# The feed-forward of a two-layer decoder step as a seven-product block form with its hidden values in DRAM, and a recurrence with one difference per level

## The chip, the core and the metric

The kernel is one inference step for 1024 prompt tokens and 8 sample tokens, in fp32, on one core of a Trainium2 chip. A core has five engines that run side by side, each with its own queue that is worked strictly in order: TensorE (PE: matmuls, with weight loads shown as PEld), VectorE (DVE), ScalarE (ACT), GpSimd (POOL) and SyncE (SP, which here only issues DMAs). They wait for each other by semaphores. The metric is device time in microseconds (us) of one execution; lower is better.

## The reference

The step has four parts: a gated linear recurrence (HGRN2), a feed-forward, latent attention (MLA), a second feed-forward. Each sits between two RMS norms.

```python
def swiglu(h, w_in, w_out):               # h is normed x: (1032, 1024)
    g, u = jnp.split(h @ w_in, 2, axis=-1)  # w_in: (1024, 2*2816)
    return (jax.nn.silu(g) * u) @ w_out     # w_out: (2816, 1024)

def hgrn2_mixer(h, s0, lb, w_in, g_norm, w_out):
    q, fz, i, gz = jnp.split(h @ w_in, 4, axis=-1)
    q = jax.nn.silu(heads(q)) * (DK_A ** -0.5)
    log_f = jnp.logaddexp(log_lb, jnp.log1p(-lbh) + jax.nn.log_sigmoid(heads(fz)))
    log_f = jnp.minimum(log_f, 0.0)
    k = -jnp.expm1(log_f)
    o, s = hgrn2_chunked(q, k, v, log_f, s0, ...)  # decays exp(b_t - b_s), b = cumsum(log_f)
    ...

for l in range(2):                        # mixer: HGRN2 in layer 0, MLA in layer 1
    x = x + rmsnorm(mixer(rmsnorm(x, g[0])), g[1])
    x = x + rmsnorm(swiglu(rmsnorm(x, g[2]), w_ffn_in[l], w_ffn_out[l]), g[3])
```

## The kernel before

**Layout.** Features lie on the 128 partitions, tokens along the free dimension. The 1032 tokens are three spans of 344 (`NS`, `W`). An fp32 product is made of three matmuls of halves in fp32r (`mm3`, L172 to 179: high x high, high x low, low x high), so each operand is split into a rounded half (a ScalarE copy) and a rest (a subtraction), for weights in `weight` (L132), for activations in `split` (L127) and `put_x` (L213).

**Feed-forward** (`ffn`, L533). For each of 22 chunks of 128 hidden columns, `inp` makes g and u for each span (8 blocks of 1024 features x 3 matmuls each, L550 and L554), multiplies by the rows' norm factor r *behind* the product (L552, L556), applies silu, multiplies (L557) and splits the result. The output product (`out_chunk`, L593) of the chunk before follows, and VectorE adds it to `acc` (L582). The last three chunks' output products stand in `outf`, together with the input product of the very last chunk, and there the closing norm runs along behind.

**Between two parts** (`finish`, L296). While the products of span s are made, `norm` of the span before it works: a first statistic `r1`, then per block of 128 features: acc times gain and r1 (L324), plus the old x that comes by DMA as `xs` (L325), the new x split as input of the next part (`put_x`), its square for the next norm factor. Then `first` gives four products of the next part that are made ahead (L360 to 363). The next part's factor r is not needed for them, since it is applied behind the product.

**Recurrent layer** (`hgrn`, L727). Eight heads, each with four projections (`proj`), the logarithm of the gate (L806 to 820), and a recurrence over blocks (`rec`). In `scaled` (L866), for each half of the tokens and each of seven levels, two differences to a reference go to VectorE (L874, L875), one exponential to ScalarE (L876) and a product to GpSimd and VectorE each (L877, L878). Projections of one head and the recurrence of the head before are dealt out by counters (`KN['pace']`).

**What sets the order.** Instructions are recorded in program order and then ordered engine by engine by a scheduler with a timeline of its own; a queue, once written, is not reordered on the chip. Tiles come from pools, and a tile that takes over a buffer waits for the buffer's last reader.

## Time and profile before

| | |
|---|---|
| median of 3 runs | 2951.73 us (2948.17 to 2955.06) |
| the profiled execution: time, span | 2951.07 us, 2949.3 us |
| TensorE | 2806.7 us busy, 95% of the span |
| weight loads | 2635.9 us, 89% |
| VectorE | 1770.6 us, 60% |
| ScalarE | 1091.2 us, 37% |
| GpSimd | 993.0 us, 34% |
| granted TensorE clock, mean | 0.976 of full speed |

The parts follow each other: the recurrent layer and its output projection to some 785 us, the first feed-forward to some 1468, then attention, the second feed-forward from some 2200 to the end. Shares over the whole span mix stages with different limits; they are read by stage. Matmuls are pipelined, so the pitch of a stream of them is read from their starts, not from their durations.

### The profile page before, as it was taken

Reading aid. Unit: us, or ns where it says so; the run is one execution under the profiler, and the core shown is the slowest. Engines: PE = TensorE matmul, PEld = TensorE weight load, DVE = VectorE, ACT = ScalarE, POOL = GpSimd, SP = SyncE. Lnnn points to the kernel's source line nnn. Section 1 sums busy time; section 2 is a strip of 40 time slices with the busy share of each in tenths; the row PEclk is TensorE's granted clock in tenths of the full one; section 3 lists DMA queues with packets and bytes.
Section 4 is the critical chain, followed back from the end, with each engine's and each line's share of the span. In section 5 each row is a group of like instructions: output and inputs, shape, how many; then the busy total and the mean of one; then the engine's idle time right before and its main releaser. Section 6 shows DMA issues by size and latency. Waiting matters only on the chain.

```text
span 2949.3 us, 54597 instructions
## 1 busy us (share of the span) xinstructions
PE 2806.7 (95%) x22360; PEld 2635.9 (89%) x22360; DVE 1770.6 (60%) x3505; ACT 1091.2 (37%) x2245; POOL 993.0 (34%) x912
## 2 busy tenths in 40 slices
PE   7988888899999999999999999978999999999998
PEld 7888888888799999999969899946889999999998
DVE  8888888873634444444357788795353444444535
ACT  6555555564431111111144666523443111111112
POOL 3455445551532322333332111242153333223330
PEclk9999999999999999999999999989999999999999
DMA  5122222144311111111132111496431111111112
GB/s 182 50 62 67 67 61 66 60 159 132 113 51 51 51 44 44 47 48 51 43 94 77 51 48 51 158 349 235 142 106 44 51 51 46 49 44 43 51 57 95
DMA packets 230970, 242.51 MB, mean 82 GB/s; under 512 B 19074, under 2 KB 211120, under 8 KB 224704
## 3 DMA queue, kind: packets, MB, share of 16 engines
q1 hardware_dynamic: 205456, 170.14, 18.9%
q0 software_dynamic: 7456, 43.00, 3.9%
q10 hardware_dynamic: 17808, 25.89, 2.5%
q8 instruction: 176, 2.88, 0.4%
q14 instruction: 74, 0.61, 0.1%
HBM read 194.87 MB, written 44.12 MB: 81 GB/s over the span
## 4 chain that ended last, share of the span: by engine, by line
PE 75%; DVE 14%; ACT 5%; issue 4%; POOL 1%; DMA 1%; SPq 0%; DVEq 0%; ACTq 0%; POOLq 0%
PE ps L177 22%; PE ps L178 22%; PE ps L179 22%; PE ps L252 2%; PE ps L1459 1%; DVE E L875 1%; DVE X L878 1%; PE ps L1386 1%; DVE E L874 1%; DVE turned L1459 1%; DVE b L826 1%; PE ps L198 1%; DVE qe L927 1%; ACT sig L830 1%; ACT w L151 1%
## 5 line engine op out<-in xcount | busy, mean ns | idle before, releaser
L177 PE MATMUL ps<-xh,w 128*128 128x344 f32 x3360 | 1105.5, 329 | 2.0 <-ACT xh L221 1.9
L178 PE MATMUL ps<-xl,w 128*128 128x344 f32 x3360 | 1084.8, 323 | 1.6 <-DVE xl L222 1.6
L179 PE MATMUL ps<-xh,w 128*128 128x344 f32 x3360 | 1080.3, 322 | 0.0
L155 POOL TENSOR_TENSOR w<-raw,w 128x512 fp32r<-128x512 f32 (+1 forms) x360 | 469.5, 1325 | 818.6 <-ACT w L151 798.9
L177 PEld LDWEIGHTS ps<-xh,w 128*128 128x128 f32 x3360 | 640.4, 191 | 25.1 <-issue 11.1
L178 PEld LDWEIGHTS ps<-xl,w 128*128 128x128 f32 x3360 | 640.5, 191 | 15.2 <-issue 8.8
L179 PEld LDWEIGHTS ps<-xh,w 128*128 128x128 f32 x3360 | 639.4, 190 | 6.0 <-issue 5.6
L582 DVE TENSOR_TENSOR acc<-ps,acc 128x344 f32<-128x344 f32 x864 | 397.5, 513 | 0.0
L151 ACT CAST w<-raw 128x1024 fp32r<-128x1024 f32 (+4 forms) x206 | 206.2, 1002 | 425.3 <-PE ps L179 325.1
L177 PE MATMUL ps<-gh,w 128*128 128x344 f32 x1056 | 338.8, 323 | 0.6 <-ACT gh L129 0.3
L179 PE MATMUL ps<-gh,w 128*128 128x344 f32 x1056 | 338.5, 321 | 0.0
L178 PE MATMUL ps<-gl,w 128*128 128x344 f32 x1056 | 338.1, 320 | 0.0
L557 POOL TENSOR_TENSOR u<-u,a 128x344 f32<-128x344 f32 x132 | 122.5, 929 | 532.8 <-DVE u L556 528.2
L556 DVE TENSOR_TENSOR u<-ps,r 128x344 f32<-128x344 f32 x132 | 68.1, 516 | 388.6 <-PE ps L179 388.4
L129 ACT CAST gh<-u 128x344 fp32r<-128x344 f32 x132 | 63.5, 481 | 504.0 <-POOL u L557 504.0
L552 DVE TENSOR_TENSOR a<-ps,r 128x344 f32<-128x344 f32 x132 | 68.1, 516 | 232.8 <-PE ps L179 226.8
L177 PEld LDWEIGHTS ps<-gh,w 128*128 128x128 f32 x1056 | 198.4, 188 | 5.6 <-issue 1.7
L178 PEld LDWEIGHTS ps<-gl,w 128*128 128x128 f32 x1056 | 198.8, 188 | 1.1 <-DVE gl L130 0.8
L179 PEld LDWEIGHTS ps<-gh,w 128*128 128x128 f32 x1056 | 198.8, 188 | 1.1 <-issue 1.1
L130 DVE TENSOR_TENSOR gl<-u,gh 128x344 fp32r<-128x344 f32 x132 | 70.1, 531 | 150.9 <-ACT gh L129 150.9
L553 ACT ACTIVATE a<-a 128x344 f32<-128x344 f32 x132 | 64.5, 490 | 224.1 <-DVE a L552 223.9
L877 POOL TENSOR_TENSOR X<-lin,E 128x256 f32<-128x256 f32 x112 | 108.9, 977 | 79.2 <-ACT E L876 48.4
(376 smaller groups left out, 4090.9 us busy)
## 6 DMA issues: line engine op xcount, KB each, us to landing
raw<-in_w_ffn_in_dram SPq DMA_DIRECT2D x88, 512.0 KB
raw<-in_w_ffn_out_dram SPq DMA_DIRECT2D x44, 512.0 KB
raw<-in_w_in_a_dram SPq DMA_DIRECT2D x32, 512.0 KB
xs<-x_d SPq DMA_DIRECT2D x72, 172.0 KB
x_d<-acc ACTq DMA_DIRECT2D x9, 1376.0 KB
x_d<-y SPq DMA_DIRECT2D x3, 1376.0 KB
od_a<-oh ACTq DMA_DIRECT2D x24, 172.0 KB
od_a<-ol ACTq DMA_DIRECT2D x24, 172.0 KB
```

Source lines behind the costliest of these rows:

```text
L130: (lo_eng or self.nc.vector).tensor_tensor(out=lo, in0=src, in1=hi, op=ALU.subtract)
L151: nc.scalar.copy(wh[:, :n], raw[:, :n])
L155: eng.tensor_tensor(out=wl[:, sl], in0=raw[:, sl], in1=wh[:, sl], op=ALU.subtract)
L177: nc.tensor.matmul(out, lhsT=wh, rhs=ah, start=first and i == 0, stop=False)
L178: nc.tensor.matmul(out, lhsT=wh, rhs=al, start=False, stop=False)
L179: nc.tensor.matmul(out, lhsT=wl, rhs=ah, start=False, stop=last and i == n - 1)
L552: nc.vector.tensor_tensor(out=a, in0=pg, in1=r[s], op=ALU.mult)
L553: nc.scalar.activation(out=a, in_=a, func=AF.Silu)
L556: nc.vector.tensor_tensor(out=u, in0=pu, in1=r[s], op=ALU.mult)
L557: nc.gpsimd.tensor_tensor(out=u, in0=u, in1=a, op=ALU.mult)
L582: nc.vector.tensor_tensor(out=acc[s][:, dc, :], in0=po, in1=acc[s][:, dc, :], op=ALU.add)
L877: nc.gpsimd.tensor_tensor(out=Xl[:, :, 0, :], in0=kl[:, :, 0, :], in1=El[:, :, 0, :], op=ALU.mult)
```

## The change

**Feed-forward.** `Gated` makes g and u from one 2 x 2 block form. The rows of a weight chunk are the halves of the 1024 features, and its two column blocks are the gate's and the up part's 128 columns, so A11, A12 (gate) and A21, A22 (up); the tokens come as two pairs of 2 x 258 (`HT`, `Q`), so B11 to B22. Seven block products (`PRODUCTS`) with sums of blocks replace eight. The weight sums S1 to S4 are made on GpSimd for each chunk; the token differences T1 to T4 and the splits of all seven token blocks are made once (`tokens`). Since blocks are mixed, x is normed *before* it is split: `put_half` writes gain x r x acc into `xn`, and `finish` makes no product ahead (`halves`). A visit is one chunk with one or both pairs: three chunks first with pair 0 alone, 19 with both, the three again with pair 1 alone. Products accumulate in two PSUM banks per pair, whose partial sums are copied out between products. The hidden values go to DRAM (`g_d`); when all are made, the output product reads them back and takes two chunks in one accumulation (`GROUP`).

**Recurrence.** `scaled` makes one difference per level, and the two signs come from two exponentials. The gate's logarithm takes six ScalarE operations and three on VectorE per half, instead of four and seven. Two small copies go to ScalarE, and the negation of f goes into a scale.

```diff
@@ finish @@
+    def put_half(s, r):
+        for pair in range(2):
+            lo, hi = max(s * W, pair * HT), min((s + 1) * W, (pair + 1) * HT)
...
+            for c in range(KC):
...
+                nc.vector.scalar_tensor_tensor(out=to, in0=acc[s][:, c, fr], scalar=g_next[:, c:c + 1], in1=r[:, fr], op0=ALU.mult, op1=ALU.mult)
...
-            xs = pool.tile([P, W], F32, name="xs", tag="xs", bufs=6)
+            xs = pool.tile([P, W], F32, name="xs", tag="xs", bufs=4 if halves else 6)
...
-            k.put_x(s, c, y, g_next)
-            if not last:
+            if not halves:
+                k.put_x(s, c, y, g_next)
+            if not last or halves:
                 s2.add(acc[s][:, c:c + 1, :], None, xs)
...
             rs[s] = yield from s2.rstd(k.new_r(s))
+            if halves:
+                yield from put_half(s, rs[s])
...
-    for i, m in enumerate(first):
+    for i, m in enumerate(() if halves else first):
@@ the new input product @@
+PRODUCTS = (("A11", "B11"), ("S1", "T1"), ("S2", "T2"), ("S4", "B22"), ("S3", "T3"), ("A12", "B21"), ("A22", "T4"))
+class Gated:
...
+        self.visits = [(f, (0,)) for f in early] + [(f, both) for f in range(len(early), NF)] + [(f, (1,)) for f in early]
...
+    def make(self, v):      # seven weight blocks of a visit
+        for i in range(2):
+            raw = k.wp.tile([P, 1024], F32, name="raw", tag="raw", bufs=2)
...
+        def total(to, a, b, op):
+            t = self.pool.tile([P, 512], F32, name="S", tag="S", bufs=2)
+            nc.gpsimd.tensor_tensor(out=t, in0=src[a], in1=src[b], op=op)
...
+            k.split(hi, lo, src[name])
...
+    def tokens(self, pair, places):
...
+            if name in how:
+                a, b = how[name]
+                nc.vector.tensor_tensor(out=src[name], in0=src[a], in1=src[b], op=ALU.subtract)
+            pool, tag = places.pop(0)
+            x = pool.tile([P, 2, KC // 2, Q], F32R, name="X", tag=tag)
+            k.split(x[:, 0], x[:, 1], src[name])
...
+    def visit(self, v, g_d):
...
+                k.mm3(to, terms, new, True, name in ("S2", "S4", "S3", "A22"))
+                if name == "A11":
+                    nc.scalar.copy(t1[p], A[p])
+                elif name == "S1":
+                    nc.scalar.copy(t5[p], C[p])
+                elif name == "S2":
+                    nc.scalar.copy(t2[p], A[p])
+                elif name == "S4":
+                    nc.vector.tensor_tensor(out=t2[p], in0=C[p], in1=t2[p], op=ALU.add)
+                    nc.scalar.activation(out=t2[p], in_=t2[p], func=AF.Silu)
+                elif name == "S3":
+                    nc.vector.tensor_tensor(out=t5[p], in0=A[p], in1=t5[p], op=ALU.add)
+                    nc.gpsimd.tensor_tensor(out=t5[p], in0=t5[p], in1=t2[p], op=ALU.mult)
+                    store(p, 1, t5[p])
...
+    def run(self, g_d):
...
+                    if v == 0:
+                        next(ta, None)
+                    elif v in (1, 2) and (v > 1 or i % 2):
+                        next(tb, None)
+                    self.ahead(v * NP_ + i + 5)
+                    next(steps)
@@ hgrn: the gate, per half @@
-                        nc.vector.scalar_tensor_tensor(out=t1, in0=x, scalar=-1.0, in1=x, op0=ALU.mult, op1=ALU.min)
-                        nc.scalar.activation(out=t1, in_=t1, func=AF.Exp)
+                        nc.scalar.activation(out=t1, in_=x, func=AF.Abs)
+                        nc.scalar.activation(out=t1, in_=t1, func=AF.Exp, scale=-1.0)
...
-                        nc.vector.tensor_scalar(out=t2, in0=t2, scalar1=hc(gt.l1), scalar2=hc(gt.loglb), op0=ALU.add, op1=ALU.max)
-                        nc.vector.tensor_tensor(out=t2, in0=t2, in1=t1, op=ALU.add)
+                        nc.vector.scalar_tensor_tensor(out=t2, in0=t2, scalar=hc(gt.loglb), in1=t1, op0=ALU.max, op1=ALU.add)
...
-                    nc.vector.tensor_scalar(out=f, in0=f, scalar1=-1.0, scalar2=None, op0=ALU.mult)
@@ rec: scaled @@
-                nc.vector.tensor_tensor(out=El[:, :, 0, :], in0=ref, in1=bl[:, :, 0, :], op=ALU.subtract)
-                nc.vector.tensor_tensor(out=El[:, :, 1, :], in0=bl[:, :, 1, :], in1=ref, op=ALU.subtract)
-                nc.scalar.activation(out=E, in_=E, func=AF.Exp)
+                nc.vector.tensor_tensor(out=pairs(E), in0=pairs(bv), in1=ref, op=ALU.subtract)
+                for i, sign in enumerate((-1.0, 1.0)):
+                    nc.scalar.activation(out=El[:, :, i, :], in_=El[:, :, i, :], func=AF.Exp, scale=sign)
...
-                nc.vector.tensor_copy(el, eb.rearrange("p (j n) -> p j n", j=CH)[:, :, P - 1])
+                nc.scalar.copy(el, eb.rearrange("p (j n) -> p j n", j=CH)[:, :, P - 1])
```

**What stands where.** TensorE's queue at the first feed-forward's entrance, before: xh and xl are the split inputs, ss the sums of squares of the last span.

```order
L177 MATMUL ps<-xh_81,w 128x344
L178 MATMUL ps<-xl_82,w 128x344
L179 MATMUL ps<-xh_81,w 128x344
L198 MATMUL ps<-ss_8832,one 128x344
L198 MATMUL ps<-ss_8840,one 128x344
L177 MATMUL ps<-xh_8041,w 128x344
L178 MATMUL ps<-xl_8042,w 128x344
```

TensorE's queue at the same place in the changed program, from the last matmul of the output projection on: sq and xs are squares for the two statistics, X the split token blocks.

```order
L184 MATMUL ps<-xh_8009,w 128x344
L257 MATMUL ps<-sq,one 32x344 x4
L257 MATMUL ps<-xs,one 32x344 x8
L203 MATMUL ps<-rs_m,one_72 128x344 x2
L257 MATMUL ps<-xs,one 32x344 x8
L203 MATMUL ps<-rs_m,one_72 128x344
L182 MATMUL ps<-X,w 128x258
L183 MATMUL ps<-X,w 128x258
```

Before, products of the feed-forward (xh, xl of another span) stand up to the last statistics; now nothing stands between the output projection and the statistics of two spans, and the first product of 258 columns comes behind them.

VectorE's queue at that place, before, from the last span's r1 on.

```order
L209 SCALAR_TENSOR_TENSOR rs_y<-rs_q,rs_y 128x344
L324 SCALAR_TENSOR_TENSOR acc<-acc,gains,rs_y 128x344 x8
L325 TENSOR_TENSOR acc<-acc,xs 128x344
L222 SCALAR_TENSOR_TENSOR xl_8042<-acc,gains,xh_8041 128x344
L325 TENSOR_TENSOR acc<-acc,xs 128x344
L222 SCALAR_TENSOR_TENSOR xl_8042<-acc,gains,xh_8041 128x344 x2
L336 TENSOR_TENSOR ss_8840<-ss_8840,xs 128x344
L222 SCALAR_TENSOR_TENSOR xl_8042<-acc,gains,xh_8041 128x344 x4
L336 TENSOR_TENSOR ss_8840<-ss_8840,xs 128x344
L222 SCALAR_TENSOR_TENSOR xl_8042<-acc,gains,xh_8041 128x344
L336 TENSOR_TENSOR ss_8840<-ss_8840,xs 128x344
L552 TENSOR_TENSOR a<-ps,r_8369 128x344
```

VectorE's queue in the changed program, from the last span's r1 on: xn is the normed input, written over by its differences.

```order
L214 SCALAR_TENSOR_TENSOR rs_y<-rs_q,rs_y 128x344
L133 TENSOR_TENSOR X<-xn,X 128x1032
L345 SCALAR_TENSOR_TENSOR acc<-acc,gains,rs_y 128x344 x8
L632 TENSOR_TENSOR xn<-xn 128x4x258
L346 TENSOR_TENSOR acc<-acc,xs 128x344 x2
L212 SCALAR_TENSOR_TENSOR rs_q<-rs_q,rs_m 128x344
L214 SCALAR_TENSOR_TENSOR r_8744<-rs_q,rs_y 128x344
L321 SCALAR_TENSOR_TENSOR xn<-acc,gains,r_8744 128x344 x8
L133 TENSOR_TENSOR X<-xn,X 128x1032 x2
L632 TENSOR_TENSOR xn<-xn 128x4x258
L133 TENSOR_TENSOR X<-xn,X 128x1032 x4
L133 TENSOR_TENSOR w<-S,w 128x512
```

Where the first use of the norm factor (a from ps and r) followed the last split, the second norm factor, eight multiplications and the wide splits now stand ahead of the first visit's fifth weight (w from S).

VectorE's queue at the gate of a head in the recurrent layer, before: tw is the gate's work tile.

```order
L810 SCALAR_TENSOR_TENSOR tw<-lin 128x516
L813 SCALAR_TENSOR_TENSOR tw<-lin,tw 128x516
L814 TENSOR_SCALAR tw<-tw,lb_580 128x516
L815 SCALAR_TENSOR_TENSOR tw<-tw 128x516
L818 TENSOR_SCALAR tw<-tw,lb_579,loglb 128x516
L793 TENSOR_TENSOR lin<-ps,r_543 128x344
L908 COPY_PREDICATED Ad_141<-lv,ps 128x128 x2
L819 TENSOR_TENSOR tw<-tw 128x516
L908 COPY_PREDICATED Ad_141<-lv,ps 128x128
L820 TENSOR_SCALAR b<-tw 128x516
```

The same place in the changed program.

```order
L1046 TENSOR_TENSOR X<-lin,E 128x256
L982 SCALAR_TENSOR_TENSOR tw<-lin,tw 128x516
L962 TENSOR_TENSOR lin<-ps,r_543 128x344
L986 SCALAR_TENSOR_TENSOR tw<-tw,loglb 128x516
L987 TENSOR_SCALAR b<-tw 128x516
L1076 COPY_PREDICATED Ad_141<-lv,ps 128x128
```

Four operations per half have left the queue, and the ones that remain take over their inputs.

## Rows read from the trace of the kernel before

**Rows 1.** windows view: us; busy PE, PEld, DVE, ACT, POOL; clock, DMA, GB/s

```profile
0.00:690.00 690.00, 610.70 (x6828) 566.61 (x6829) 573.57 (x1046) 377.04 (x684) 330.11 (x277) 0.94 0.30 93
...
785.00:795.00 10.00, 3.53 (x10) 2.33 (x9) 7.99 (x12) 4.01 (x6) 6.11 (x6) 0.67 0.35 123
...
795.00:1468.00 673.00, 672.79 (x4286) 672.50 (x4285) 295.37 (x622) 133.62 (x215) 216.67 (x187) 1.00 0.17 50
...
1468.00:1580.00 112.00, 106.34 (x563) 82.50 (x562) 70.55 (x115) 54.48 (x112) 36.40 (x31) 0.97 0.30 95
...
2193.00:2203.00 10.00, 3.49 (x8) 2.57 (x9) 7.63 (x12) 5.00 (x6) 5.98 (x6) 0.76 0.31 105
...
2203.00:2850.00 647.00, 647.00 (x4116) 647.00 (x4115) 289.64 (x612) 127.96 (x207) 204.57 (x179) 1.00 0.17 50
```

**Rows 2.** the same view, inside the first feed-forward.

```profile
1000.00:1400.00 400.00, 400.00 (x2550) 400.00 (x2550) 184.57 (x394) 71.10 (x107) 122.71 (x107) 1.00 0.16 47
```

**Rows 3.** the same view, one head of the recurrent layer.

```profile
203.04:279.14 76.10, 67.35 (x807) 62.50 (x807) 66.56 (x119) 40.92 (x74) 39.01 (x32) 0.96 0.22 65
```

**Rows 4.** timeline, 256-column products: start, duration, engine, line, operation.

```profile
1773.33 0.28 PE L178 MATMUL ps<-PTl,vh 128*128 128x256 f32 x1
...
1775.95 0.28 PE L179 MATMUL ps<-w,cl 128*128 128x256 f32 x1
...
1773.45 0.19 PEld L177 LDWEIGHTS ps<-PTh,vh 128*128 128x128 f32 x1
...
1773.57 0.19 PEld L178 LDWEIGHTS ps<-PTl,vh 128*128 128x128 f32 x1
```

**Rows 5.** weight preparation by line, 800 to 1400: busy us, mean ns, idle.

```profile
L151 ACT CAST w<-raw 128x1024 fp32r<-128x1024 f32 x54 | 56.9, 1055 | 168.0 <-PE ps L179 144.9 <-DMA raw<-in_w_ffn_in_dram 23.2
...
L155 POOL TENSOR_TENSOR w<-raw,w 128x512 fp32r<-128x512 f32 x107 | 136.4, 1296 | 208.7 <-ACT w L151 208.7
```

**Rows 6.** timeline at the second feed-forward's entrance, and one from 1512.

```profile
1512.87 1.29 DVE L155 TENSOR_TENSOR w<-raw,w 128x512 fp32r<-128x512 f32 x2 [0.56 <-ACT w L151]
...
2157.94 2.61 SPq L323 DMA_DIRECT2D xs<-x_d  x4
...
2177.20 0.74 PE L198 MATMUL ps<-rs_m,one 128*128 128x344 f32 x2
...
2180.63 6.71 DVE L324 SCALAR_TENSOR_TENSOR acc<-acc,gains,rs_y 128x344 f32<-128x344 f32 x8
...
2198.86 0.50 DVE L552 TENSOR_TENSOR a<-ps,r 128x344 f32<-128x344 f32 x1
...
2199.29 0.50 DVE L556 TENSOR_TENSOR u<-ps,r 128x344 f32<-128x344 f32 x1
```

**Rows 7.** VectorE by line, 0 to 690: count, busy us, mean ns, idle.

```profile
L874 DVE TENSOR_TENSOR E<-b 128x256 f32<-128x256 f32 x112 | 84.7, 756 | 4.1 <-POOL kt L925 1.2 <-POOL X L877 1.0
...
L875 DVE TENSOR_TENSOR E<-b 128x256 f32<-128x256 f32 x112 | 64.9, 579 | 0.0
...
L923 DVE TENSOR_TENSOR E<-b 128x512 f32<-128x512 f32 x16 | 16.8, 1048 | 0.0
...
L820 DVE TENSOR_SCALAR b<-tw 128x516 f32<-128x516 f32 x16 | 14.1, 878 | 0.0
...
L813 DVE SCALAR_TENSOR_TENSOR tw<-lin,tw 128x516 f32<-128x516 f32 x16 | 11.1, 692 | 12.9 <-ACT tw L812 12.9
...
L834 DVE SCALAR_TENSOR_TENSOR lin<-lin,sig 128x1032 f32<-128x1032 f32 x8 | 9.8, 1226 | 0.0
...
L973 DVE COPY qpad<-lin 128x8 f32<-128x8 f32 x8 | 7.0, 869 | 0.0
```

**Rows 8.** timeline of one weight load and its cast, 1013 to 1019.

```profile
1013.89 8.15 SPq L148 DMA_DIRECT2D raw<-in_w_ffn_in_dram  x2
...
1017.96 1.05 ACT L151 CAST w<-raw 128x1024 fp32r<-128x1024 f32 x1 [1.87 <-DMA raw<-in_w_ffn_in_dram]
```

**Rows 9.** windows view, same head, the gate's tile alone: VectorE, ScalarE.

```profile
203.04:279.14 76.10, 10.46 (x14) 5.08 (x8) 0.96 0.22 65
```

More of the change, by code (lines that the diff above doesn't have):

```diff
@@ L25 @@
 W = T // NS
+HT = T // 2
+Q = HT // 2
 FF = 2816
@@ L162, in open_pre, with mm3 @@
     def open_pre(self):
-        self.pre, pool = self.right("pre", 2)
-        return pool
+        self.pre = self.right("pre", 2)
+        return self.pre[1]
     def close_pre(self):
         if self.pre is not None:
-            self.pre.close()
+            self.pre[0].close()
             self.pre = None
-    def mm3(self, out, terms, first=True, last=True):
+    def mm3(self, out, terms, first=True, last=True, more=False):
         nc = self.nc
         n = len(terms)
+        skip = {"skip_group_check": True} if more else {}
         for i, ((wh, wl), (ah, al)) in enumerate(terms):
-            nc.tensor.matmul(out, lhsT=wh, rhs=ah, start=first and i == 0, stop=False)
-            nc.tensor.matmul(out, lhsT=wh, rhs=al, start=False, stop=False)
-            nc.tensor.matmul(out, lhsT=wl, rhs=ah, start=False, stop=last and i == n - 1)
+            nc.tensor.matmul(out, lhsT=wh, rhs=ah, start=first and i == 0, stop=False, **skip)
+            nc.tensor.matmul(out, lhsT=wh, rhs=al, start=False, stop=False, **skip)
+            nc.tensor.matmul(out, lhsT=wl, rhs=ah, start=False, stop=last and i == n - 1, **skip)
     def xterm(self, k, s):
@@ L302, in finish @@
     rs = [None] * NS
+    def put_half(s, r):
+        for pair in range(2):
+            lo, hi = max(s * W, pair * HT), min((s + 1) * W, (pair + 1) * HT)
+            if lo >= hi:
+                continue
+            if pair not in k.xn:
+                k.xn[pair] = [k.xpool[1].tile([P, KC // 2, HT], F32, name="xn", tag=f"x{i}{pair}") for i in "hl"]
+            for c in range(KC):
+                to = k.xn[pair][c // 4][:, c % 4, lo - pair * HT:hi - pair * HT]
+                fr = slice(lo - s * W, hi - s * W)
+                nc.vector.scalar_tensor_tensor(out=to, in0=acc[s][:, c, fr], scalar=g_next[:, c:c + 1], in1=r[:, fr], op0=ALU.mult, op1=ALU.mult)
+                if c % 2:
+                    yield
     def products(s):
@@ L338, in norm @@
         nc.scalar.dma_start(out=x_d[s], in_=acc[s])
-        if not last:
+        if not last or halves:
             for _ in range(lags[1]):
@@ new lines, in ffn, with fetch @@
+        gp = st.enter_context(tc.tile_pool(name="gp", bufs=2, reuse_waits="tile"))
+        G, wo = {}, {}
+        order = [*range(LAST, NF), *range(LAST)]
+        def fetch(n):
+            f = order[n]
+            if f not in G:
+                t = gp.tile([P, 2, T], F32R, name="G", bufs=4)
+                nc.sync.dma_start(out=t.bitcast(F32), in_=g_d[f])
+                for s in range(NS):
+                    G[f, s] = tuple(t[:, i, s * W:(s + 1) * W] for i in range(2))
+                G[f] = t
+                wo[f] = k.weight(w_out[f * P:(f + 1) * P, :].unsqueeze(1), 1, D, None, gp if n % 2 else None)
@@ new lines, in ffn @@
+        fetch(0)
+        fetch(1)
+        acc = [k.new_acc() if k.accs is not None and s < NS - 1 else accp.tile([P, KC, W], F32, name=f"acc{s}") for s in range(NS)]
+        k.x_tiles(k.xpool[1], range(NS - 1))
+        k.x_tiles(k.xpool2[1], [NS - 1])
+        f = 0
+        while f < NF - LAST:
+            fs = range(f, min(f + (GROUP if f else 1), NF - LAST))
+            for s in range(NS):
+                for dc in range(KC):
+                    if dc == 0 and s < 2:
+                        fetch(fs[-1] + 1 + s)
+                    po = out_chunk(k, wo, G, [order[n] for n in fs], s, dc)
+                    if f == 0:
+                        nc.scalar.copy(acc[s][:, dc, :], po)
+                    else:
+                        nc.vector.tensor_tensor(out=acc[s][:, dc, :], in0=po, in1=acc[s][:, dc, :], op=ALU.add)
+            f = fs[-1] + 1
@@ L584, in outf @@
+        for f in range(NF - LAST, NF):
+            fetch(f)
         def outf(s, dc):
-            if dc == 0:
-                next(units[NF - 1])
-            po = out_chunk(k, wo, G, range(NF - LAST, NF), s, dc)
+            po = out_chunk(k, wo, G, order[NF - LAST:], s, dc)
             nc.vector.tensor_tensor(out=acc[s][:, dc, :], in0=po, in1=acc[s][:, dc, :], op=ALU.add)
```

194 lines of the change are left out of this document (123 added, 71 removed).

## The prediction

> **What bounds the kernel now.** I read the busy time by stage first, then single stretches of the timeline. In [rows 1] TensorE is busy 672.8 of 673 us from 795 to 1468 and all 647 us from 2203 to 2850: these are the two feed-forwards, and nothing but TensorE's own pitch bounds them. [rows 2] gives the pitch of the 344-column products: 2550 matmuls in 400 us, 156.9 ns each. At both entrances TensorE stands: between 785 and 795 it ran 10 matmuls and between 2193 and 2203 only 8 [rows 1], where 64 fit, so each entrance loses about 8.5 us now. In the recurrent layer, 0 to 690, VectorE is the densest engine. One head there lasts 76.1 us, with VectorE busy 66.6, TensorE 67.4 (latencies counted), ScalarE 40.9 and GpSimd 39.0 [rows 3].
>
> **The products.** Per 128 hidden columns the old input product runs 2 x 3 x 8 x 3 = 144 matmuls of 344 columns: 144 x 0.1569 = 22.6 us. The new form runs 7 products x 2 token pairs x 4 x 3 = 168 matmuls of 258 columns. The nearest row is the 256-column product of the attention: 23 starts from 1773.33 to 1775.95, 2.62 us for 22 steps, 119.1 ns [rows 4]; two more columns at the slope between the two widths (37.8 ns for 88) make 120.0. So 20.2 us. A layer has 3696 such matmuls for 3168: 443.5 for 497.1 us, twice -53.6 = **-107**. The output product keeps its 1584 matmuls of 344.
>
> The load of a matrix lasts 0.19 us, starts while a matmul runs, and the next starts 0.12 us later [rows 4], so loads lie under each other and under matmuls. The Trainium skill (TensorE: Matmul & The Clock Gate, The mechanism) says that a load overlaps a running matmul only where they use different row groups. By that rule loads would be paid on top of the streams and the -107 would be lost, 3020 where the rows give 2913; the trace disagrees.
>
> **Inside a two-pair visit** (19 a layer, 20.2 us each) the other engines have room. ScalarE: 7 casts of 512 (half of the 1.06 us in [rows 5]) and 14 small copies, casts and Silus of 258 at some 0.4: 9.5 us. VectorE: 7 subtractions of 512 at 0.65 and 12 of 258 at some 0.4: 9.4. GpSimd: 4 weight sums at 1.30 [rows 5] and two products at some 0.75: 6.7. A bank that is added to again rests three products, 4.3 us, while a copy takes 0.4. I charge 0.15 us a visit for single late copies, **+6**; from 0 (it only adds waits) to the price in the slower rival.
>
> **The entrance of the feed-forward** is where the gain goes back. Today x is multiplied by the weights before the norm is known: the old queue goes from the last xl to r's first use, and the matmuls of chunks 0 and 1 fill TensorE meanwhile. Now x must be normalised first, split and differenced, and all of that stands on VectorE. By the order of the changed program, the second pass over span 1 starts only at the end of the output projection. Behind that end VectorE has:
> - span 1: eight multiplications, 6.7 us as now [rows 6]; the last four additions wait for xs buffers (4, not 6), which the statistics must have read and a load of 2.6 us [rows 6] must refill; then statistics and rstd, of which 3.4 us are seen from its matmul at 2177.20 to the next multiplication [rows 6]. About 14.
> - 16 half-width multiplications at 0.25 (0.43 for 344 back to back in [rows 6], less 172 columns), three operations over 1032 columns at 1.2 (L834 in [rows 7]), two small ones: 8.5.
> - span 2: 6.7, one of 1.2, two additions, and the same tail, later, because one addition stands behind all eight multiplications: 18.
> - eight multiplications (3.4), seven operations of 1032 (8.4), three weight subtractions (2.0; two halves took 1.29 in [rows 6]): 14.
>
> That is 54.5 us until the first visit's fifth weight is there. Visits 1 and 2 then put ten operations of 1032, eleven of 512 and eleven of 258 on VectorE: 12 + 7.2 + 4.7 = 24, to 79, and TensorE has three products (4.3) behind them: 83 us for work of 252 x 0.12 = 30.2. Lost 53, less today's 8.5: +44 an entrance, **+88**. Low end: both tails hidden, 16 less each, +56. High end: the 22 wide operations at the crowded rate, as L874 with 0.76 on average against 0.43 for a wider one alone [rows 6, 7], +0.8 each: +123.
>
> **Smaller terms.** The last three one-pair visits take 84 x 0.12 = 10.1 us, but the way from one visit's last weight to the next one's is a load of 4.1 us [rows 8], four GpSimd sums in a row (5.2) and some 3 us of casts and subtractions: 12.2. Two of them show it in each layer: **+8** (0 to 20). From the last input product to the first output product the hidden values come back from DRAM: the loads of later chunks hide, the first waits for tiles that the last visits free: **+8** (0 to 20). The last hidden chunk's 48 matmuls a span (7.5 us) no longer lie over the final norms: two spans, 15 us, at the step to the attention layer, which already has TensorE busy 106.3 of 112 [rows 1]; I take 12, and 3 at the end: **+15** (0 to 30). The doubled chain of the output product spares VectorE only, which is not late there.
>
> **The recurrent layer.** Of VectorE's work per head: the gate's 14 operations (10.46 us) [rows 9] become 6, in each half two like L813 (0.69) and one like L820 (0.88): 4.5, so -6.0. The negation of 1032 columns goes (an estimate of 0.7, below the 1.2 of L834, which reads two operands), qpad (0.87) and two el of four columns (at some 0.4) go to ScalarE. The 14 pairs of differences (0.76 + 0.58) become one of 512, as L923: 1.05 [rows 7]: -4.0. Together -12 of 66.6. ScalarE gets 4 gate steps of 0.635 (5.08 us for 8) [rows 9], 14 more exponentials and three copies, some 6 us on 40.9; it stays at two thirds. What is late next is TensorE: 288 x 0.157 = 45.2 us of projections, and the remaining 519 small ones bring its busy time to 67.4 [rows 3]. So a head can fall to 67 at best, and some of the twelve lies beside TensorE already; I take 7 of the 9 that are open, x 8 = **-56** (-16, if the longer ScalarE chain eats most, to -85).
>
> Sum: -107 + 6 + 88 + 8 + 8 + 15 - 56 = -38. The profiled execution took 2951.07 us (span 2949.3), the median is 2951.73, so nothing is to be corrected: **2913 us**.
>
> **Rivals.**
> 1. Shorter entrances. For it: most of the 54 us are waits in series that another order of events would fold. Against it: the queue is strictly in order. Low end of the entrances (-32) and a recurrent layer that reaches TensorE's floor (-16 more): about 2865.
> 2. Slower: ScalarE's queue stops TensorE. For it: casts of weights stood 145 us behind TensorE between 800 and 1400 (L151 in [rows 5]), waiting for a buffer. Today only later casts queue behind them. Now the copies that release a PSUM bank stand in that queue; a cast that waits for a two-product tile (5.7 us) outlasts the 4.3 us of rest by 1.4, twice a visit, 2.9 x 38 = +109, so 3021. It decides from 38/38 = 1.0 us a visit. Against it: three tiles of two halves, and the order puts the copies of both pairs ahead of the casts.
> 3. TensorE is paced by the number of loads: then 168 matmuls cost 168/144 of 22.6 = 26.4, +165 instead of -107: 3185. [rows 4] speak against it.
> 4. Entrances at their high end (+35) with the recurrent layer at its low end (+40): 2988.
> 5. The terms cancel: within 6 us of 2951.
>
> **How the numbers follow.** The forecast as written, 2880 to 2945: 43 in 100. Rival 1 and beyond: 23. Rival 5: 9. Slower: rival 2 12, rival 4 11, rival 3 2. So faster 0.66, same 0.09, slower 0.25; about 0.2%, 6 us, is what can be told from no change. The range takes the forecast, most of rival 1 and up to rival 4's middle: 2850 to 2980. The forecast's own is 2880 to 2945.
>
> **What would show it.** Right: 258-column matmuls at 119 to 121 ns and TensorE at 100% in the two-pair visits; two holes of over 40 us in TensorE's work behind the projections with VectorE full; heads of 67 to 71 us. Wrong: waits of TensorE for ScalarE copies within visits; entrances under 30 us; heads still at 75. The sign turns if the entrances cost over 63 us each beyond today's, or if a visit needs 21.3 us.

## The result and the profile after

The changed kernel takes 3018.79 us (median of 4 runs, 3012.62 to 3027.33) against 2950.74 us before: ratio 1.0231, 95% interval 1.0202 to 1.0261. Forecast were 2913 us and a range of 2850 to 2980; it came out slower. The profiled execution took 3021.40 us, its span is 3019.6 us, 70.3 longer than before.

The windows view of the changed kernel, cut where the work changes hands (columns as in [rows 1]):

```profile
728.40:772.56 44.16, 18.47 (x48) 4.24 (x47) 27.95 (x43) 14.63 (x29) 17.55 (x15) 0.63 0.32 104
...
772.56:833.00 60.44, 43.35 (x255) 39.83 (x254) 45.90 (x59) 31.26 (x53) 19.44 (x12) 0.76 0.26 76
...
833.00:1225.90 392.90, 387.24 (x3195) 384.54 (x3194) 207.01 (x361) 168.10 (x399) 135.59 (x117) 1.00 0.34 102
...
1225.90:1271.50 45.60, 38.19 (x254) 35.95 (x252) 24.82 (x40) 18.95 (x42) 15.06 (x13) 0.85 0.39 116
...
1271.50:1283.90 12.40, 0.20 (x3) 0.07 (x1) 1.19 (x3) 2.71 (x4) 6.38 (x6) 0.67 0.91 302
...
2189.90:2233.30 43.40, 17.19 (x47) 3.46 (x47) 25.98 (x43) 14.85 (x29) 16.05 (x15) 0.55 0.31 106
...
2233.30:2290.90 57.60, 42.43 (x255) 39.20 (x254) 48.70 (x59) 30.64 (x52) 16.95 (x11) 0.81 0.35 104
```

The first row goes from the last product of the output projection to the first product of the feed-forward: 44.2 us without a product, at a granted clock of 0.63. In the second, the three one-pair visits take 60.4 us for 252 matmuls, 30.2 us of work. The 19 two-pair visits (third row) are nearly full, the last three one-pair visits take 45.6 us for 30.2, and the 12.4 us to the output product are empty. The last two rows are the same entrance in the second layer. Before, the way from the last product of the output projection to the end of two chunks' input products lasted 60.1 us, with 288 products of 344 columns (45.2 us) and 20 matmuls for statistics in it, so 15 were lost:

```profile
749.40:809.50 60.10, 53.63 (x308) 48.24 (x307) 30.98 (x43) 25.74 (x46) 28.58 (x25) 0.94 0.39 129
```

From the same cuts in both layers, the sum beside the forecast (us; entrances less 2 x 15):

| term | forecast | measured |
|---|---|---|
| input product at its pitch | -107 | -107 |
| waits inside two-pair visits | +6 | +17 (9.8 and 7.4) |
| two entrances | +88 | +115 (74.4 and 70.8 lost) |
| last one-pair visits | +8 | +29 (15.4 and 13.2) |
| to the output product | +8 | +23 (12.4 and 10.8) |
| norms behind the feed-forward, end | +15 | +14 (what is left) |
| recurrent layer | -56 | -21 |
| sum | -38 | +70 |

The first row of the table takes 0.120 us a matmul, the median distance of their starts; what single ones lost beyond that is in the second row.

The row of the norms is only what the others leave, and the trace puts it elsewhere than the forecast did. At the step to the attention layer nothing more is lost: its statistics come 23.2 us later than before, as the first feed-forward's last output product already does (1533.8 before, 1557.0 now). At the attention's output projection they come 31.8 us later (L198 before, L203 now):

```profile
1548.81 0.84 PE L198 MATMUL ps<-rs_m,one 128*128 128x344 f32 x2
1572.03 0.84 PE L203 MATMUL ps<-rs_m,one 128*128 128x344 f32 x2
...
2130.79 0.85 PE L198 MATMUL ps<-rs_m,one 128*128 128x344 f32 x2
2162.58 0.84 PE L203 MATMUL ps<-rs_m,one 128*128 128x344 f32 x2
```

So 8.9 of the 14 us are lost inside the attention layer, most of them around its output projection, where TensorE now waits for squares (2099 to 2190; us, times, longest) and did not before; 0.8 lie in the first feed-forward's output products and 4.6 in the second's.

```profile
PE ps L257 <- ACT sq L246: 4.6, 2, 3.0
```

What causes these 8.9 us is open: the same stretch, from the last output product to the end of the attention's output projection, took 632.9 us here, and 626.5 and 638.7 in two runs below that do not edit it (`tail`, `early2`).

The pitch was right. Four visits of the second layer, 672 matmuls of 258 columns in 81.0 us, 120.5 ns each with their small waits (forecast 120.0, [rows 4]):

```profile
2333.40:2414.40 81.00, 81.00 (x675) 80.97 (x674) 42.92 (x76) 35.30 (x84) 27.27 (x25) 1.00 0.35 105
```

Five heads of the recurrent layer, 74.1 us each against 76.3 in five heads before; VectorE busy 60.6 a head for 66.6 ([rows 3]):

```profile
117.12:487.49 370.37, 333.44 (x4037) 311.92 (x4036) 303.23 (x467) 228.09 (x480) 200.36 (x160) 0.93 0.22 66
```

VectorE's groups by line, 0 to 690, which answer to [rows 7] (count, busy us, mean ns, idle before and what ended it); the last row is of the kernel before:

```profile
L1042 DVE TENSOR_TENSOR E<-b 128x512 f32<-128x512 f32 x112 | 104.5, 948 | 2.9 <-POOL X L1045 1.2
...
L962 DVE TENSOR_TENSOR lin<-ps,r 128x344 f32<-128x344 f32 x66 | 33.5, 508 | 32.5 <-PE ps L184 32.5
...
L1001 DVE SCALAR_TENSOR_TENSOR lin<-lin,sig 128x1032 f32<-128x1032 f32 x8 | 14.1, 1758 | 15.6 <-ACT sig L997 15.6
...
L793 DVE TENSOR_TENSOR lin<-ps,r 128x344 f32<-128x344 f32 x66 | 33.4, 506 | 1.9 <-PE ps L179 1.8
```

The one difference of 512 columns (L1042) takes 0.95 us where two took 0.76 + 0.58. But operations that nobody edited got longer: the same scaling of q is L834 with 1226 ns before and L1001 with 1758 here. And VectorE now waits 32.5 us for projections (L962), where it waited 1.9 before (L793).

The timeline of TensorE behind the first product of the feed-forward, which starts at 772.56 (start, duration, operation):

```profile
773.49 0.42 PE L184 MATMUL ps<-X,w 128*128 128x258 f32 x1
...
773.71 0.42 PE L182 MATMUL ps<-X,w 128*128 128x258 f32 x1
...
777.62 0.28 PE L183 MATMUL ps<-X,w 128*128 128x258 f32 x1
...
777.73 0.28 PE L184 MATMUL ps<-X,w 128*128 128x258 f32 x1
```

After 44 us with little work the matmuls of 258 columns start 0.215 us apart, and from 777.5 on 0.12. The granted clock was 0.50 from 740 to 772.56 and 0.51 from there to 777.5, the level of 1.2 GHz. In the two entrances 146 of 504 matmuls ran at the slow pitch (in unbroken runs of four or more), 14 us more; in the last visits 60 (5.6 us): some 19 us in all. In the two-pair visits, where the granted clock is 1.00, no such run stands. The forecast priced the waits, but not the slow matmuls behind them.

The entrance on VectorE, with the waits in brackets, and a row of GpSimd:

```profile
728.31 7.27 DVE L345 SCALAR_TENSOR_TENSOR acc<-acc,gains,rs_y 128x344 f32<-128x344 f32 x8
...
744.49 0.52 DVE L212 SCALAR_TENSOR_TENSOR rs_q<-rs_q,rs_m 128x344 f32<-128x344 f32 x1 [7.05 <-ACT rs_q L211]
...
745.67 5.02 DVE L321 SCALAR_TENSOR_TENSOR xn<-acc,gains,r 128x172 f32<-128x172 f32 x16
...
754.90 5.94 DVE L345 SCALAR_TENSOR_TENSOR acc<-acc,gains,rs_y 128x344 f32<-128x344 f32 x8
...
774.84 0.52 DVE L212 SCALAR_TENSOR_TENSOR rs_q<-rs_q,rs_m 128x344 f32<-128x344 f32 x1 [11.29 <-ACT rs_q L211]
...
776.03 3.99 DVE L321 SCALAR_TENSOR_TENSOR xn<-acc,gains,r 128x344 f32<-128x344 f32 x8
...
787.94 0.69 DVE L133 TENSOR_TENSOR w<-S,w 128x512 fp32r<-128x512 f32 x1
```

```profile
793.81 3.86 POOL L603 TENSOR_TENSOR S<-raw 128x512 f32<-128x512 f32 x1 [23.30 <-DMA raw<-in_w_ffn_in_dram]
```

It is the queue that was forecast: span 1's second pass at the output projection's end, statistics (7.05 us of waiting), `xn`, span 2's pass, statistics (11.29), `xn`, then splits to the first visit's fifth weight, done at 788.6, 60 us behind 728.4 (forecast 54.5). What was not forecast comes after it: the second visit's first weight sum waits until 793.81 for its load, since the first visit's last parts free the raw buffers so late (`entr`, below, loads it earlier).

### The profile page after: what moved, and what is told of

Read it like the earlier page. It is cut to its first block, busy times and chain, and to the rows that moved or that the text cites. A ratio compares the mean times of both kernels' runs of the same rounds, so it can differ in the third digit from the quotient of the medians.

```text
span 3019.6 us, 58495 instructions
## 1 busy us (share of the span) xinstructions
PE 2754.1 (91%) x23444; PEld 2558.2 (85%) x23444; DVE 1893.6 (63%) x3402; ACT 1329.0 (44%) x3010; POOL 986.2 (33%) x886
## 5 line engine op out<-in xcount | busy, mean ns | idle before, releaser
L182 PE MATMUL ps<-X,w 128*128 128x258 f32 x2464 | 714.7, 290 | 45.1 <-ACT w L132 23.0
L184 PE MATMUL ps<-X,w 128*128 128x258 f32 x2464 | 703.8, 288 | 10.9 <-DVE w L133 10.7
L183 PE MATMUL ps<-X,w 128*128 128x258 f32 x2464 | 706.6, 287 | 1.4 <-DVE X L133 1.4
L182 PEld LDWEIGHTS ps<-X,w 128*128 128x128 f32 x2464 | 476.6, 193 | 56.5 <-ACT w L132 27.1
L184 PEld LDWEIGHTS ps<-X,w 128*128 128x128 f32 x2464 | 475.3, 194 | 15.2 <-DVE w L133 15.1
L183 PEld LDWEIGHTS ps<-X,w 128*128 128x128 f32 x2464 | 478.1, 194 | 2.5 <-DVE X L133 2.0
L158 POOL TENSOR_TENSOR w<-raw,w 128x512 fp32r<-128x512 f32 x184 | 238.9, 1319 | 616.0 <-ACT w L154 609.0
L182 PE MATMUL ps<-xh,w 128*128 128x344 f32 x1248 | 423.6, 340 | 3.9 <-ACT xh L226 2.5
L183 PE MATMUL ps<-xl,w 128*128 128x344 f32 x1248 | 407.7, 327 | 1.6 <-DVE xl L227 1.6
L184 PE MATMUL ps<-xh,w 128*128 128x344 f32 x1248 | 402.7, 324 | 0.0
L182 PE MATMUL ps<-G,w 128*128 128x344 f32 x1056 | 344.0, 326 | 25.6 <-DMA G<-g_d 25.5
L183 PE MATMUL ps<-G,w 128*128 128x344 f32 x1056 | 341.8, 324 | 0.0
L184 PE MATMUL ps<-G,w 128*128 128x344 f32 x1056 | 340.1, 322 | 0.0
L133 DVE TENSOR_TENSOR w<-S,w 128x512 fp32r<-128x512 f32 x200 | 209.5, 1056 | 148.4 <-ACT w L132 147.3
L182 PEld LDWEIGHTS ps<-xh,w 128*128 128x128 f32 x1248 | 240.0, 192 | 20.9 <-issue 8.6
L183 PEld LDWEIGHTS ps<-xl,w 128*128 128x128 f32 x1248 | 240.2, 192 | 13.3 <-issue 6.7
L184 PEld LDWEIGHTS ps<-xh,w 128*128 128x128 f32 x1248 | 239.6, 192 | 2.4 <-issue 2.2
L182 PEld LDWEIGHTS ps<-G,w 128*128 128x128 f32 x1056 | 201.3, 191 | 31.0 <-issue 29.2
```

Of the source, the lines that this page charges most:

```text
L133: (lo_eng or self.nc.vector).tensor_tensor(out=lo, in0=src, in1=hi, op=ALU.subtract)
L158: eng.tensor_tensor(out=wl[:, sl], in0=raw[:, sl], in1=wh[:, sl], op=ALU.subtract)
L182: nc.tensor.matmul(out, lhsT=wh, rhs=ah, start=first and i == 0, stop=False, **skip)
L183: nc.tensor.matmul(out, lhsT=wh, rhs=al, start=False, stop=False, **skip)
L184: nc.tensor.matmul(out, lhsT=wl, rhs=ah, start=False, stop=last and i == n - 1, **skip)
```

## Experiments

Chips differ by half a per cent, so times are compared as ratios to the kernel before on the same chip, with 95% intervals.

### Which half of the change costs

`hgrn_only` puts the new recurrence into the kernel before, `gated_only` the old recurrence into the changed kernel.

> The kernel before with the new recurrence alone (one difference per level, six ScalarE and three VectorE operations at the gate, the small copies on ScalarE); the feed-forwards as before. Theory (the stages add up): the recurrent layer and its output projection got shorter by 21 us in the trace of the changed kernel, heads of 73.3 instead of 75.7 us, because VectorE's operations became fewer but the chain of a head passed to TensorE; so some 2930 us, 20 to 22 less than before. Rival (the new feed-forward disturbs the recurrent layer, by its weight loads and its place in the order): without it the predicted heads of 69 us appear, some 2895 us.

> The changed kernel with the recurrence of the kernel before; feed-forwards in the seven-product form. Theory (the stages add up): both feed-forwards cost 48 and 38 us more than before and the way around attention 4, so 2951 + 91 = some 3040 us, recurrent heads at 75.7 us. Rival (the edits disturb each other): under 3025 us.

Measured: 0.9927 (0.9913 to 0.994), 2927.82 us, and 1.0313 (1.0295 to 1.0331), 3042.16 us. Both theories held, the halves add up: the recurrence gives 19 us, the feed-forwards cost 95.

### Why the recurrence gives so little

`two_mm` leaves a matmul out, `x_dve` moves an operation (both on `hgrn_only`).

```diff
 two_mm, head projections
-            nc.tensor.matmul(out, lhsT=wh, rhs=al, start=False, stop=False)
 x_dve
-                nc.gpsimd.tensor_tensor(out=Xl[:, :, 0, :], in0=kl[:, :, 0, :], in1=El[:, :, 0, :], op=ALU.mult)
+                nc.vector.tensor_tensor(out=Xl[:, :, 0, :], in0=kl[:, :, 0, :], in1=El[:, :, 0, :], op=ALU.mult)
```

> The kernel before with the new recurrence alone, and the head projections made of two matmuls per block instead of three (the product of the weights' rounded half with the tokens' rest is left out): 96 matmuls of 344 columns less per head, 15 us of TensorE. Theory (with the new recurrence the chain of a head lies mostly on TensorE, 40 of 75 us of the chain followed back in the changed kernel against 29 before, with the projections the largest part): heads fall by 7 to 11 us, in all 55 to 90 us less than the new recurrence alone, 2840 to 2872. Rival (VectorE, lengthened by GpSimd beside it, still bounds the head): heads fall by under 3 us, 2905 or more.

> The kernel before with the new recurrence alone, and the product of keys with the decays (14 of 128x256 per head, about 1.05 us each on GpSimd) moved to VectorE. Theory (an operation of VectorE that reads two tensors from SBUF takes 0.41 us alone and 0.9 to 1.35 while GpSimd works, so GpSimd's share costs VectorE more than it takes off it): VectorE gets 14 x 0.41 = 5.8 us more work per head, but its lengthened operations shrink by about as much; its busy time per head stays within 3 us and the heads get no longer, 2900 to 2930. Rival (VectorE's time just adds up): heads longer by 3 to 6 us, 2950 to 2975.

`two_mm`: 0.9907 (0.9892 to 0.9922), heads 72.2 us for 73.9. The theory fell and the rival held: TensorE's busy time got 10 us shorter a head and the head only 1.6. The matmuls left out were worth 15 us at full clock; the granted clock of the five heads was 0.87, for 0.94 in `hgrn_only`. Five heads of it, and VectorE's waits in 110:480:

```profile
117.26:478.42 361.16, 281.08 (x3548) 254.69 (x3549) 305.52 (x465) 240.80 (x495) 192.60 (x160) 0.87 0.23 68
```

```profile
DVE tw L826 <- ACT tw L825: 24.1, 11, 3.1
...
DVE lin L839 <- ACT sig L836: 12.1, 6, 2.2
...
DVE lin L802 <- PE ps L199: 0.6, 1, 0.6
```

VectorE no longer waits for projections (0.6 us), but for ScalarE in the gate (24.1) and in the sigmoid (12.1). Its busy time is the same 61.1 us a head, and it waits 11 us where it waited 13.

`x_dve`: 0.9898 (0.9883 to 0.9913), heads 72.2, as the theory had it. VectorE has 14 operations more a head and is busy 59.9 us instead of 61.1. The two products of a level, both on VectorE now:

```profile
L876 DVE TENSOR_TENSOR X<-lin,E 128x256 f32<-128x256 f32 x112 | 72.3, 646 | 3.4 <-PE ps L903 1.3 <-PE ps L887 1.0 <-ACT E L875 0.9
...
L877 DVE TENSOR_TENSOR X<-lin,E 128x256 f32<-128x256 f32 x112 | 65.4, 584 | 0.1
```

The product that stayed on VectorE falls from 955 ns in `hgrn_only` to 584. Sorted by what GpSimd did meanwhile, 100 to 560 us of the kernel before: L878 took 413 ns on average where GpSimd worked for at most a tenth of the operation (17 of them) and 906 where it worked for nine tenths or more (32), L874 414 (55) and 1351 (18), but L793, which reads one operand from PSUM, 508 (24) and 505 (22). So the time of VectorE's operations on two tensors in SBUF depends on how much GpSimd runs beside them. The Trainium skill (SBUF — State Buffer, SBUF: two separate sides) says that a VectorE operation with two SBUF inputs and a GpSimd operation that reads SBUF lock each other out for a whole instruction; these rows agree.

`diff_only` and `gate_only` split the recurrence's edits (diffs as in the change above).

> The kernel before with one edit of the recurrence alone: one difference of 512 columns per level and two exponentials in place of two differences and one exponential; gate and small copies as before. Theory (VectorE, stretched by GpSimd, bounds the head, and the new gate's longer run on ScalarE gives nothing back): most of the new recurrence's 19 us come from here, 2 us a head, ratio to before 0.993 to 0.996. Rival (the gate brings the gain, the shorter differences only slide under GpSimd): ratio 0.998 or more.

> The kernel before with the other edits of the recurrence alone: the gate in six operations of ScalarE and three of VectorE per half, the small copies on ScalarE, the negation in a scale; two differences per level as before. Theory (the gate's links on ScalarE stand in series, so VectorE saves 6 us a head but waits as long for them): ratio to before 0.998 to 1.001. Rival (VectorE's saved work counts wherever it stands): ratio 0.994 or less.

Measured: 0.9991 (0.9982 to 1.0001) and 0.991 (0.9897 to 0.9924). Both theories fell and both rivals held: the gate and the small copies give all of it and the single difference nothing. Five heads of `diff_only`, 75.9 us each:

```profile
126.90:506.30 379.40, 339.85 (x4034) 316.16 (x4034) 322.45 (x525) 213.20 (x440) 199.24 (x162) 0.94 0.22 65
```

VectorE is busy 64.5 us a head for 66.6, 2.1 less for 14 operations less, and its waits grow by 1.7.

`sig_split` asks whether the gate gains by the sigmoid that it makes in two parts; `gate_x` joins `gate_only` and `x_dve`; `pace7` and `pace9` shift the recurrence of `hgrn_only`.

```diff
 sig_split
-                    nc.scalar.activation(out=sig[:, :n, :], in_=lin[:, :n, :], func=AF.Sigmoid)
+                    nc.scalar.activation(out=sig[:, 0, :], in_=f, func=AF.Sigmoid)
+                    nc.scalar.activation(out=sig[:, 1:n, :], in_=lin[:, 1:n, :], func=AF.Sigmoid)
 pace7, pace9
-    'pace': (8, 26, 13),
+    'pace': (7, 26, 13),    # or (9, 26, 13)
```

> The kernel before with one edit: the sigmoid over f, q and the last head's output gate (3096 columns, 2.8 us on ScalarE) made as two operations, f first. Theory (VectorE waits 6.0 us a head for this sigmoid, and that wait is the gate's gain): the wait falls to 3 or 4 us, heads 2 to 3 us shorter, ratio to before 0.992 to 0.995. Rival (the gain comes from VectorE's eight operations less per head): ratio 0.998 or more.

> The kernel before with the new gate and small copies, two differences per level as before, and the keys' products on VectorE instead of GpSimd. Theory (GpSimd beside VectorE takes away what fewer operations give): VectorE's busy time per head stays within 3 us of the 62.3 of the new gate alone though it gets 14 operations more, ratio to before 0.986 to 0.991. Rival (the operations add up): heads 3 to 6 us longer than with the new gate alone, ratio 0.998 or more.

> The kernel before with the new recurrence alone, and the recurrence of a head recorded one step of twelve earlier against the projections. Theory (the waits of VectorE for projections, 4.8 us a head, come from where the two are dealt): the head moves by 1 us or more either way, ratio to before below 0.990 or above 0.995. Rival (the run through the engines is fixed by dependencies): ratio 0.991 to 0.995, as without the shift.

> The kernel before with the new recurrence alone, and the recurrence of a head recorded one step of twelve later against the projections. Theory (the waits for projections come from where the two are dealt; with less work on VectorE a later start fits better): ratio to before below 0.990. Rival (fixed by dependencies): ratio 0.991 to 0.995, as without the shift.

`sig_split`: 1.0035 (1.0021 to 1.0048), a miss. The wait moved to the second part and grew elsewhere:

```profile
DVE lin L835 <- ACT sig L831: 24.3, 5, 4.9
...
DVE tw L813 <- ACT tw L812: 11.4, 6, 3.3
```

So the sigmoid in two parts is not the gain. What is left is that VectorE has fewer operations at the gate and the small copies (busy 62.3 us a head in `gate_only` for 66.6); that is concluded by exclusion, no run takes these edits apart. `gate_x`: 0.9872 (0.9857 to 0.9887), 2927.35 us against 2964.18, the lowest ratio here and what its theory had; VectorE busy 61.8 us a head with heads of 71.1:

```profile
115.52:471.10 355.58, 330.51 (x4035) 309.38 (x4034) 309.05 (x608) 220.89 (x410) 133.05 (x90) 0.96 0.23 69
```

`pace7`: 1.0078 (1.0063 to 1.0094); `pace9`: 1.0441 (1.0425 to 1.0457), heads of 95.4 us with VectorE busy 52.9:

```profile
102.46:579.42 476.96, 348.81 (x4037) 325.71 (x4036) 264.25 (x465) 280.74 (x520) 191.17 (x161) 0.84 0.17 52
```

Neither direction helps, and `pace9`'s theory had the sign wrong. But one step of twelve moves a head by 7 or 22 us, so the rival fell too: where the recurrence stands among the projections moves a head more than any edit of an engine's work did here.

### The entrance

`rate4` records more steps of the norm under the output projection; `entr` loads the second visit's weights early; `early2` makes two one-pair visits of three.

```diff
 rate4, for 'hgrn' and 'mla'
-'rate': 2
+'rate': 4
 entr, in Gated.run
+                    if v == 0 and i == 0:
+                        self.raws[1] = self.load(1, "X5")
 early2
-        early = range(3)
+        early = range(2)
```

> The changed kernel, with four steps of the norm recorded after each product of the output projections instead of two. Theory (the norm of span 1 stands behind the output projection because normed input takes more than the 14 steps that a span's products record): the second statistics of span 1 move under the output projection of span 2, the two stretches from the end of an output projection to the first two-pair visit shorten from 104 and 101 us to some 85 to 90, in all 25 to 35 us less than the changed kernel, 2985 to 2995. Rival (the statistics then stop TensorE inside the output projection, and the normed input of span 2 still sets the start): within 8 us of the changed kernel.

> The changed kernel; the raw weights of the second visit of each feed-forward are loaded at its start into a token tile that is needed later, and the tiles of pair 1 are taken in another order for it. Theory (visits 1 and 2 wait for weights because the second visit's load starts only when the first visit's last part has freed the two raw buffers, its first sum being made 65 us after the output projection's end): the three first visits fall from 60 and 57 us to 48 to 54, in all 10 to 20 us less, some 3004. Rival (VectorE's queue of splits and differences sets the pace): the wait passes to VectorE's parts and the visits stay within 3 us.

> The changed kernel with two chunks instead of three in the one-pair visits at the start and at the end. Theory (a one-pair visit costs 15 us at the end and 20 at the start for 10 us of matmuls, since its weights are made in series by GpSimd, ScalarE and VectorE for half the matmuls): one visit less at either end of both feed-forwards, some 5 us less at the end and 0 to 8 at the start, each; 2993 to 3010. Rival (at the start the visits only fill the wait for VectorE's splits of pair 1): the start of the first two-pair visit waits instead, 3015 to 3035.

`rate4`: 1.0202 (1.0186 to 1.0218), some 9 us less than the changed kernel. Its windows in the first layer (end of the recurrent layer and output projection, then the two stretches of the entrance):

```profile
640.00:738.20 98.20, 95.22 (x549) 78.28 (x548) 38.58 (x70) 39.87 (x83) 21.12 (x19) 1.00 0.36 116
...
738.20:762.80 24.60, 10.12 (x27) 2.27 (x26) 13.82 (x17) 8.91 (x17) 7.21 (x7) 0.70 0.18 60
...
762.80:821.00 58.20, 41.58 (x254) 38.58 (x253) 46.62 (x59) 30.72 (x52) 18.59 (x11) 0.81 0.29 84
```

The 44.2 us without a product became 24.6, as the theory had it. But the output projection ended at 738.2 instead of 728.4, and in the second layer the way from the first feed-forward to that point took 648.6 us for 632.8. So of the 38 us gained in both layers' first stretches some 26 came back as a longer way there, the rival's part.

`entr`: 1.017 (1.0155 to 1.0185). The first visits fell to 55.9 and 55.1 us (from 60.4 and 57.6), between theory and rival. Its trace is 12.0 us shorter than the changed kernel's: 7 us from these visits, and 6.8 from the way to the second layer's output product, which neither had expected (see the part on why the prediction was wrong). TensorE's waits in the first layer's visits (us, times, longest), in the changed kernel and in `entr`:

```profile
PE ps L182 <- ACT w L132: 8.1, 3, 3.4
...
PE ps L184 <- DVE w L133: 2.0, 3, 0.8
```

```profile
PE ps L184 <- DVE w L133: 5.6, 3, 3.7
...
PE ps L182 <- ACT w L132: 2.2, 2, 1.8
```

The wait for ScalarE's casts went, and the one for VectorE's parts behind them took over half of it.

`early2`: 1.0148 (1.0135 to 1.0162), some 24 us less, as the theory had it. Cut at the same 252 matmuls, the entrances take 100.2 and 95.5 us for 104.6 and 101.0, the last ones 41.3 and 40.2 for 45.6 and 43.5: a one-pair visit costs more than its matmuls at both ends.

### The last visits

`tail` loads the raw weights of the last two visits into token tiles of pair 0.

```diff
+                    if v == len(self.visits) - 3 and i == 0:
+                        for u, tags in ((v + 1, ("X0", "X1")), (v + 2, ("X2", "X3"))):
+                            self.raws[u] = self.load(u, tags)
```

> The changed kernel; the raw weights of the last two one-pair visits are loaded early, into token tiles of pair 0 that no product needs any more, instead of waiting for the two raw buffers. Theory (the last visits wait for load, sums, cast and subtraction one after the other, since a raw buffer comes free only with the last part of a visit): the three last visits, 45 and 43 us now for 30 of matmuls, fall to 33 to 37, in all 15 to 22 us less, some 3000. Rival (GpSimd's four sums and the casts set the pace, not the loads): within 5 us of the changed kernel.

Measured: 1.0252 (1.0237 to 1.0268), no gain. The theory fell. The last visits took 43.3 and 45.0 us. TensorE's waits in the first layer's, changed kernel and `tail`:

```profile
PE ps L182 <- ACT w L132: 4.0, 4, 1.6
...
PE ps L184 <- DVE w L133: 2.9, 5, 1.3
```

```profile
PE ps L184 <- DVE w L133: 3.4, 3, 2.2
...
PE ps L182 <- ACT w L132: 2.5, 2, 1.5
...
PE ps L182 <- ACT t L676: 1.5, 2, 0.9
...
PE ps L182 <- ACT t L682: 0.9, 2, 0.5
```

The loads were issued at 1210 and done before these visits began at 1223, and the waits for weights went from 6.9 to 5.9 us and passed to ScalarE's copies of partial sums (2.4): in a one-pair visit a bank rests for one product only. So not the loads but the making of the weights, and with it the copies, which stand in the same ScalarE queue, set the pace there, as the rival had it.

### Together

`combo2` joins `early2`, `entr` and `x_dve`; `combo_r3` adds three steps of the norm instead of two.

> The changed kernel with two chunks in the one-pair visits, the second visit's weights loaded early, and the keys' products on VectorE. Theory (the three gains come from different stretches and add up, the two at the entrance in part): ratio to before 1.015 for the two chunks, less 0.2 to 0.5% for the early weights, less 0.3% for the products, 1.006 to 1.011. Rival (the two changes at the entrance take away the same wait): 1.012 or more.

> The same as combo2, with three steps of the norm recorded after each product of the output projections instead of two. Theory (with three steps the norm of span 1 moves half under the output projection, with less of a stop there than with four): 6 to 15 us less than combo2, ratio to before 1.001 to 1.007. Rival (what moves under the output projection stops TensorE there for as long): within 4 us of combo2.

Measured: 1.0099 (1.0084 to 1.0115) and 1.0072 (1.0058 to 1.0086). `combo2` lies in its theory's range, so the gains add up in the main; `combo_r3` gains 8 us more, as its theory had it, and ends just above the ratio it named. The seven products stay behind the kernel before. Since `gate_x` stands at 0.9872, they would have to find another 2%.

## Why the prediction was wrong

**Right.** The price of the seven products (-107), and with it the dismissal of the rival that loads pace TensorE. The entrance's mechanism, VectorE's queue in strict order, to within 6 us up to the fifth weight. Rival 2, ScalarE stopping TensorE in the visits, stayed small: all that the 38 visits lost is 17 us, not 109, and the wait lists put only 3.1 of it down to ScalarE.

**Right by luck.** The norms (+15, measured +14). The forecast put 12 of them at the step to the attention layer, where nothing was lost; most of the 14 came in the attention layer itself, which the sum had left out.

**The step that failed most** is the recurrent layer: "a head can fall to 67 at best, and some of the twelve lies beside TensorE already; I take 7 of the 9 that are open". It was 2.2 of 9. The twelve us were worked out from durations of operations as they stood beside GpSimd; VectorE's busy time fell by 6, because what remained slid further under GpSimd's unchanged 39 us. And TensorE's busy time is no floor that the head runs to: `two_mm` lowered it by 10 us and the head followed by 1.6. The measured 21 lies inside the term's own bounds (16 to 85), at the low end, where one should have gone with a row of L874 at 756 ns in view, which takes 414 beside an idle GpSimd. A contrast of this kind stood in the prediction, but only for the entrance, and its 0.43 was that of an operation with a PSUM operand (L552), the kind that GpSimd does not lengthen.

**The entrances** (+88, measured +115) were inside their bounds up to 123. Missing were the slow matmuls (14 us) and the second visit's weights, which `entr` shows to be worth some 7 us in the visits; the queue itself was 6 us longer in the first layer. The miss would show larger, had today's loss not been taken at 8.5 us an entrance, from one window of 10 us, where it is 15: the new entrances lose 145 us in all, for 106 in the forecast.

**The last visits and the way to the output product** (+8 each, measured +29 and +23) were outside theirs of 20. The price of the visits was taken from load, sums and casts in series as if only two of three showed; the slow clock adds 5.6, and `tail` shows that without the loads the copies are next. For the way to the output product only the wait for the tiles was counted:

```profile
1271.38 0.28 PE L184 MATMUL ps<-X,w 128*128 128x258 f32 x1
...
1276.08 3.04 SPq L729 DMA_DIRECT2D G<-g_d  x4
...
1283.86 0.63 PE L182 MATMUL ps<-G,w 128*128 128x344 f32 x1 [12.20 <-DMA G<-g_d]
```

TensorE stands until hidden values come back, and the load of 1 MB is issued only at 1276.08, after the last product. No run was made to load it earlier, but `entr` does so by chance in the second layer: there the load is issued at 2714.21, 5 us before the last input product, and the way takes 4.0 us instead of 10.8.

```profile
2714.21 0.42 SPq L740 DMA_DIRECT2D G<-g_d  x1
...
2723.39 0.39 PE L182 MATMUL ps<-G,w 128*128 128x344 f32 x1 [3.87 <-DMA G<-g_d]
```

All these misses went the same way. The terms were priced as single values with gains at their likeliest and losses near their floor. The high ends of the entrances, the last visits, the way and the norms, the low end of the recurrence and the two firm terms, -107 + 6 + 123 + 20 + 20 + 30 - 16 = +76, are nearer to the +70 than the sum of the values taken; the range stopped at 2980.

## What to carry to other kernels

A form that saves matmuls pays where TensorE is full, and there the saving can be forecast to a few microseconds. What it costs sits at its ends, where its input must be complete before the first product. The longer waits there are paid twice, as waits and as slow matmuls behind them (7 of the 74 us lost in the first entrance); the short waits in the two-pair visits left the granted clock at 1.00. Before counting on fewer VectorE operations, look at how long the same operation takes with and without GpSimd beside it: moving work from GpSimd to VectorE shortened VectorE's busy time and the head here. And in a loop that several engines share, an engine's busy time need not be a floor that the loop reaches.

## What was not expected of the hardware

An operation of 256 columns on two tensors in SBUF takes VectorE 0.41 us with GpSimd idle and 0.9 to 1.35 with GpSimd at work beside it, and one of 344 columns with a PSUM operand 0.51 either way. TensorE's 258-column matmuls start 0.215 us apart behind a stretch with few matmuls, at a granted clock of 0.51, and 0.12 at full clock; the slow ones cost some 19 us in this kernel.
